# Order of transposes, scores and fillers in a stick-breaking attention loop, and of one projection's accumulators

## The chip, the cores and the metric

The kernel runs on one core of a Trainium2 chip. The core has a matrix engine (TensorE, PE in the profile, with PEld for its weight loads), a vector engine (VectorE, DVE), an activation engine (ScalarE, ACT), a general one (GpSimd, POOL), and a sync engine (SP) that issues most DMAs. The metric is the device time of one execution in microseconds (us); lower is better. The time before is the median of three runs.

## The reference

One layer of a model, in float32, with 1024 rows (positions) of width 1024. The input is normalised and modulated by a conditioning vector, then projected. Sixteen heads of 64 columns mix the positions: eight by forgetting attention (softmax with a decay) and eight by stick-breaking attention. Each is gated, and all go through one output projection, a gated residual and a last normalisation. The part that the change is about is the stick-breaking half:

```python
z = q @ k.T * scale                      # per head
strict = k_pos < q_pos
log_keep = where(strict, log_sigmoid(-z), 0.0)
later = cumsum(log_keep, reverse) - log_keep
w = where(strict, exp(log_sigmoid(z) + later), 0.0)
out = (w @ v) * silu(g)
```

Read as products, a weight is sigmoid(z) times the product of sigmoid(-z) over all later keys up to the query.

## The kernel before, in words

Heads are worked in eight pairs: 0 to 3 stick-breaking, 4 to 7 forgetting attention. A **unit** (p, h, i) is one head h of pair p and one block i of 128 queries, with its i+1 blocks of 128 keys. There are 16 units in a pair, 128 in all; `units` lists them and k counts them. Within pair 0 the order is blocks 0 to 3 of both heads and then 4 to 7 of both, so that units 8 to 15 are all wide. Float32 operands are split into a rounded high part and a low part, so that a product is two or three faster matrix products.

For a stick-breaking unit the steps are these.

- `att_scores` (L447): TensorE computes the scores into S, the only score buffer, in PSUM (L459, L460). ScalarE takes sigmoid(-z) as kp and sigmoid(z) as be (L481, L483), both reading S. VectorE scans kp from the end, in one or two pieces (L488, L492). GpSimd multiplies be by the shifted scan (L494) and clears the diagonal (L495). The function returns the last ScalarE and VectorE instructions of the unit.
- `att_query` (L428): a copy of the next unit's query block for the low-part product (L433).
- `att_transpose` (L499): TensorE transposes the weights by blocks of 128 into one or two groups of up to four, in buffers T (two of them, L511). ScalarE copies the high halves (L513), VectorE takes the low ones (L514); the last of these is kept in `lows`. Between the first and the second group, or behind the only one, it calls `att_pv` for pairs of units that are ready.
- `att_pv` (L521): the value products of two query blocks of a head into the one value buffer (L528), then the sums: a ScalarE copy (L535), two VectorE adds (L536, L537), GpSimd's product with the gate (L538) and a store.

The **fillers** are a chain of generators: the projections of later pairs (`gen_m`, `gen_v`), some small gate work, splitting the output weights, and the last gate projection (`gen_last_g`, L977). Each step of one issues some twelve wide-row value matmuls or six of 512 columns. `want` spreads the steps over the turns. Projections are accumulated in `acc` buffers, two of them in PSUM, which ScalarE and VectorE empty (`evac_m`). Weights come by DMA and are split on GpSimd (L126, L127).

The loop makes one **turn** per k. A turn issues scores of unit k, about half of its fillers, transposes of unit k-2 (LAG is 2) with value products, and the other fillers. Four turns also empty a part of the first projections that was held back in an SBUF tile (`HELD`: k = 4, 5, 6, 10; by `evac_q`, L265, or `evac_k`, L274, one head's half each). From turn 116 on the output projection is mixed in.

The order on TensorE is the program's. On ScalarE, VectorE and GpSimd a planner orders instructions by readiness and program order; `after(...)` (L83) makes a block's instructions stand behind the given ones on their engine.

Of the kernel before, what the change touches and what calls it, by code (L numbers as in the profile page):

```python
# [16 lines left out]
NB = 8  # L17
# [10 lines left out]
def tile_hybrid_layer(  # L28
# [33 lines left out]
    def acc_tile(name):  # L62
        return ps.tile([P, 512], F32, tag="acc", bufs=2, name=name)
# [19 lines left out]
    def after(*instructions):  # L83
        stack = ExitStack()
        for i in instructions:
            stack.enter_context(tc.issue_after(i.ins))
        return stack
# [177 lines left out]
    def evac_q(p, ch, acc, qst, heads):  # L265
        s = slice(ch * 512, ch * 512 + 512)
        for h in heads:
            r = slice(h * HD, h * HD + HD)
            o = slice((1 - h) * HD, (1 - h) * HD + HD)
            nc.scalar.activation(qst[h][r, s], acc[r, :], AF.Copy, scale=SCALE)  # L270
            nc.vector.scalar_tensor_tensor(qst[h][o, s], acc[r, :], SCALE, qst[h].bitcast(F32)[r, s],
                                           op0=ALU.mult, op1=ALU.subtract)

    def evac_k(p, ch, acc, kst, klo, heads):  # L274
        s = slice(ch * 512, ch * 512 + 512)
        for h in heads:
            r = slice(h * HD, h * HD + HD)
            o = slice((1 - h) * HD, (1 - h) * HD + HD)
            first = nc.scalar.copy(kst[h][r, s], acc[r, :])
            if ch == 1 and p in (2, 4, 6):  # L280
                key_casts[:] = [first]
            kf = kst[h].bitcast(F32)
            nc.sync.dma_start(kf[o, s], kf[r, s])
            last = nc.vector.tensor_tensor(klo[r, s], acc[r, :], kf[r, s], op=ALU.subtract)  # L284
        return first, last

    def evac_g(p, ch, acc, sg):
        s = slice(ch * 512, ch * 512 + 512)
        nc.scalar.activation(sg[:, s], acc, AF.Tanh, scale=0.5)
        nc.vector.scalar_tensor_tensor(sg[:, s], sg[:, s], 1.0, acc, op0=ALU.add, op1=ALU.mult)  # L290
# [22 lines left out]
    def evac_m(p, m, ch, acc, heads=(0, 1)):  # L313
        if m == 0:
            evac_q(p, ch, acc, qst[p], heads)
        elif m == 1:
            return evac_k(p, ch, acc, kst[p], klo[p], heads)
        else:
            evac_g(p, ch, acc, sgt[p])
# [115 lines left out]
    masks, scaled, lows = [], [], []  # L435

    def att_causal(u):
        p, h, i = u
        if p >= 4:
            if not masks:  # L440
                masks.append(pv_tile("causal_ps", 1)[:, :P])
                nc.vector.tensor_copy(masks[0], causal)
            f = fb[2 * (p - 4) + h]
            dg = slice(i * P, i * P + P)
            nc.vector.tensor_tensor(f[:, dg], f[:, dg], masks[0], op=ALU.add)
# [53 lines left out]
    def att_transpose(u, between=()):  # L499
        p, h, i = u  # L500
        a = st_w.pop(u)
        j, qo = i // 2, (i % 2) * P
        for g in range((i // 4) + 1):
            n = min(4, i + 1 - 4 * g)
            if (p, h, j, g) not in st_pt:
                st_pt[p, h, j, g] = pt_tile(f"pt_{p}_{h}_{j}_{g}", F32R, [P, 2, 4, 256])
            hi, lo = (st_pt[p, h, j, g][:, x] for x in range(2))
            tp = t_tile(f"T_{p}_{h}_{i}_{g}")
            for b in range(n):
                kb = 4 * g + b  # L510
                nc.tensor.transpose(tp[:, b * P:(b + 1) * P], a[:, kb * P:(kb + 1) * P], ident)  # L511
            t3 = tp[:, :n * P].rearrange("p (a b) -> p a b", a=n)
            nc.scalar.copy(hi[:, :n, qo:qo + P], t3)  # L513
            lows[:] = [nc.vector.tensor_tensor(lo[:, :n, qo:qo + P], t3, hi.bitcast(F32)[:, :n, qo:qo + P],  # L514
                                               op=ALU.subtract)]
            while between:
                att_pv(*between.pop(0))

    y_last = []

    def att_pv(p, h, j):  # L521
        acc = pv_tile(f"pv_{p}_{h}_{j}")
        last = 2 * j + 1
        acc2 = acc.rearrange("p (a b) -> p a b", a=2)
        for kb in range(last + 1):
            pt = st_pt[p, h, j, kb // 4][:, :, kb % 4]
            q0 = P if kb == last else 0
            nc.tensor.matmul(acc2[:, :, q0:], vt[p][:, kb, h * P:(h + 1) * P], pt[:, :, q0:],  # L528
                             start=(kb == 0), stop=(kb == last))
        r = slice(h * HD, h * HD + HD)  # L530
        o = slice((1 - h) * HD, (1 - h) * HD + HD)
        qs = slice(j * 256, j * 256 + 256)
        ty = sb.tile([P, 512], F32, tag="ty", bufs=2, name=f"ty_{p}_{h}_{j}")
        tm, yt = ty[:, :256], ty[:, 256:]
        nc.scalar.copy(tm[r, :], acc[o, :256])  # L535
        nc.vector.tensor_tensor(yt[r, :], acc[r, :256], tm[r, :], op=ALU.add)  # L536
        nc.vector.tensor_tensor(yt[r, :], acc[r, 256:], yt[r, :], op=ALU.add)  # L537
        nc.gpsimd.tensor_tensor(yt[r, :], yt[r, :], sgt[p][r, qs], op=ALU.mult)  # L538
        if p == NPAIR - 1:
            if not y_last:  # L540
                y_last.extend([big("sg", 2, "y7h", F32R), big("kl", 2, "y7l", F32R)])
            yh, yl = y_last
            nc.scalar.copy(yh[r, qs], yt[r, :])
            nc.gpsimd.tensor_tensor(yl[r, qs], yt[r, :], yh.bitcast(F32)[r, qs], op=ALU.subtract)
        else:
            nc.sync.dma_start(y_dr[p, r, qs], yt[r, :])
# [258 lines left out]
    for kb in range(NB):  # L805
# [9 lines left out]
        if kb < len(evacs):  # L815
            n, h = evacs[kb]
# [4 lines left out]
    held = att_tile("st_held")  # L821
# [31 lines left out]
    def load_wo(pr):  # L853
        hi = big(f"u{pr}", 1, f"woh_{pr}", F32R)
        lo = big(f"v{pr}", 1, f"wol_{pr}", F32R)
        nc.sync.dma_start(hi.bitcast(F32), wo_dr[0, pr])
        nc.sync.dma_start(lo.bitcast(F32), wo_dr[1, pr])
        wo[pr] = (hi, lo)
# [118 lines left out]
    def gen_last_g(p):  # L977
        tiles = fetch_m(p, 2)
        yield
        make_g(p)  # L980
        accs = [acc_tile(f"m_{p}_2_{ch}") for ch in range(2)]
        for kt in range(NB):
            for ch in (1, 0):
                m_step(accs[ch], tiles, kt, ch)
            if kt == NB - 1:
                for ch in (1, 0):
                    evac_m(p, 2, ch, accs[ch])
            load_wo(kt)
            yield

    fillers = chain([
# [10 lines left out]
    LEAD = 2  # L1002
    LAG = 2
# [4 lines left out]
    HELD = {4: (1, 1), 5: (0, 0), 6: (1, 0), 10: (0, 1)}  # L1008
# [4 lines left out]
    def fill(want):  # L1013
        while done[0] < want:
            done[0] += 1
            next(fillers, None)
# [10 lines left out]
    units = [u for p in range(NPAIR) for u in order(p)]  # L1027
    want = [0.0]
# [10 lines left out]
    seen = set()  # L1039
    ready = []  # L1040
    LAST = 16 * (NPAIR - 1)
    tail = chain([gen_out_first(6), gen_out_last(6)] + [gen_out(t) for t in OUT_ORDER[1:]])
    fill(2)
    for k in range(len(units) + LAG + 1):
        if k < len(units):
            if k == 16 * 4 - 1:
                load_fb(0)
                load_fb(1)
            if k == 0:
                att_query(units[0])  # L1050
            issued = att_scores(units[k], units[k + 1] if k + 1 < len(units) else None)
            if k == 16 * 4 - 1:
                att_causal(units[k + 1])
            if k + 1 < len(units):
                att_query(units[k + 1])
            p, h, i = units[k]
            if 4 <= p < NPAIR - 1 and i == 0:
                load_fb(2 * (p - 4) + h + 2)
        fill(want[2 * k + LEAD + 1])
        if LAG <= k < len(units) + LAG:  # L1060
            u = units[k - LAG]
            att_transpose(u, ready)
            if k in HELD:
                m, h = HELD[k]
                with after(*issued, *lows):
                    evac_m(0, m, 1, held[:, m * 512:(m + 1) * 512], (h,))
            seen.add(u)
            if (u[0], u[1], u[2] ^ 1) in seen:
                ready.append((u[0], u[1], u[2] // 2))
        while k >= len(units) + LAG and ready:  # L1070
            att_pv(*ready.pop(0))
        fill(want[2 * k + LEAD + 2])
        if k >= LAST + OUT0:
            for _ in range(TAIL[min(k - LAST - OUT0, len(TAIL) - 1)]):
                next(tail, None)
        if k == LAST:
            load_y(6)
            load_ln()
        for i, d in enumerate(YLOAD):
            if k == LAST + d:  # L1080
                load_y(OUT_ORDER[i + 1])
# [64 lines left out]
```

## Time and profile before

| | |
|---|---|
| median of three runs | 687.88 us (687.73 to 688.04) |
| the profiled execution | 687.36 us |
| its span, first to last instruction | 685.6 us |
| mean granted clock of TensorE | 0.997 |
| stick-breaking turns | from the first scores at 80.70 us to about 345 us |
| busy: DVE, ACT, POOL | 71%, 56%, 59% |

In the profile a row of a timeline gives the start in us, the length in us, the engine, the line of the kernel, the operation, what it writes and reads, the shapes and a count; a bracket at its end gives the time for which the engine stood idle ahead of it and what ended that. [...]

### The profile page before, as it was taken

How to read it: one execution, taken by the hardware profiler on the slowest of the kernel's cores; microseconds unless marked ns; L12 is line 12 of the kernel's file. 1: busy time of each engine (PE TensorE's matmuls, PEld its weight loads, DVE VectorE, ACT ScalarE, POOL GpSimd, SP SyncE). 2: the span in 40 equal slices, each digit the busy share in tenths (PEclk: the TensorE clock that was granted, in tenths of full speed). 3: DMA queues.
4: the chain of work that ended last, by engine and by line, in shares of the span. 5: the costliest groups of instructions: out<-in, count | busy, mean ns of one | idle time of the engine just before them, and what ended most of it. 6: DMA issues, size and time to landing. Idle time of an engine off the chain costs nothing.

```text
span 685.6 us, 11206 instructions
## 1 busy us (share of the span) xinstructions
PE 671.9 (98%) x3713; PEld 571.4 (83%) x3713; DVE 488.1 (71%) x996; ACT 381.5 (56%) x857; POOL 403.3 (59%) x529
## 2 busy tenths in 40 slices
PE   8999999999999999999999999999999999999995
PEld 5788888788998888889988888889988878888885
DVE  6697779867668777777776675766676777885645
ACT  6567378756568666566665564655565666521000
POOL 5560269756347565556368878777784365655411
PEclk9999999999999999999999999999999999999998
DMA  8973432112102122122123454254352297143301
GB/s 334 409 280 129 138 75 77 40 25 62 32 10 70 40 55 55 40 54 55 52 88 128 162 164 164 79 176 147 125 163 64 68 361 287 59 179 102 119 32 61
DMA packets 45272, 81.54 MB, mean 119 GB/s; under 512 B 5216, under 2 KB 19360, under 8 KB 44960
## 3 DMA queue, kind: packets, MB, share of 16 engines
q1 hardware_dynamic: 43632, 76.54, 33.7%
q10 hardware_dynamic: 1584, 4.31, 1.9%
q8 instruction: 29, 0.48, 0.3%
q14 instruction: 27, 0.22, 0.1%
HBM read 60.34 MB, written 16.29 MB: 112 GB/s over the span
## 4 chain that ended last, share of the span: by engine, by line
PE 85%; DVE 6%; ACT 3%; POOL 2%; issue 2%; DMA 1%; DVEq 0%; POOLq 0%; ACTq 0%
PE pv L528 9%; PE m L296 9%; PE m L298 9%; PE m L297 9%; PE T L511 8%; PE o L909 4%; PE o L908 4%; PE o L907 4%; PE S L460 4%; PE S L459 4%; PE v L356 4%; PE v L354 4%; PE v L355 3%; PE st_q L614 1%; PE st_late L614 1%
## 5 line engine op out<-in xcount | busy, mean ns | idle before, releaser
L296 PE MATMUL m<-uh,whi 128*128 128x512 f32 x304 | 125.0, 411 | 0.7 <-DVE kl L284 0.7
L514 DVE TENSOR_TENSOR pt<-T,pt 128x512 fp32r<-128x512 f32 (+2 forms) x192 | 103.2, 551 | 26.0 <-ACT pt L513 24.2
L298 PE MATMUL m<-uh,wlo 128*128 128x512 f32 x304 | 119.7, 394 | 0.0
L297 PE MATMUL m<-ul,whi 128*128 128x512 f32 x304 | 119.6, 394 | 0.0
L513 ACT CAST pt<-T 128x512 fp32r<-128x512 f32 (+2 forms) x192 | 88.7, 479 | 42.8 <-PE T L511 39.9
L494 POOL TENSOR_TENSOR be<-be,kp 128x127 f32<-128x127 f32 (+3 forms) x64 | 77.6, 1213 | 37.5 <-DVE kp L492 27.6
L488 DVE TENSOR_TENSOR_SCAN kp<-kp,floor 128x512 f32<-128x512 f32 (+2 forms) x64 | 65.1, 1018 | 28.5 <-ACT kp L481 25.4
L528 PE MATMUL pv<-pt,v 128*128 128x512 f32 x320 | 82.8, 388 | 0.3 <-DVE pt L514 0.3
L538 POOL TENSOR_TENSOR ty<-ty,sg 64x256 f32<-64x256 f32 x64 | 46.9, 733 | 42.7 <-DVE ty L537 18.3
L475 POOL TENSOR_SCALAR a<-a,l 128x1024 f32<-128x1024 f32 (+3 forms) x64 | 48.1, 752 | 39.6 <-DVE l L473 28.9
L298 PEld LDWEIGHTS m<-uh,wlo 128*128 128x128 f32 x304 | 57.1, 188 | 13.6
L459 PE MATMUL S<-k,q 128*128 128x512 f32 (+5 forms) x192 | 66.2, 346 | 0.3 <-DVE nm L467 0.2
L296 PEld LDWEIGHTS m<-uh,whi 128*128 128x128 f32 x304 | 57.2, 188 | 10.1 <-DVE kl L284 1.1
L460 PE MATMUL S<-kl,qz 128*128 128x512 f32 (+5 forms) x192 | 65.3, 341 | 0.0
L472 ACT ACTIVATE a<-a,nm 128x1024 f32<-128x1024 f32 (+3 forms) x64 | 49.8, 778 | 26.8 <-DVE nm L467 25.8
L297 PEld LDWEIGHTS m<-ul,whi 128*128 128x128 f32 x304 | 57.3, 189 | 7.9
L528 PEld LDWEIGHTS pv<-pt,v 128*128 128x128 f32 x320 | 55.4, 189 | 9.6 <-DVE pt L514 0.6
L481 ACT ACTIVATE kp<-S 128x128 f32<-128x128 f32 (+3 forms) x64 | 41.7, 652 | 33.6 <-PE S L460 31.2
L467 DVE CUSTOM_DVE_ANT_0 a<-S,fb 128x1024 f32<-128x1024 f32 (+3 forms) x64 | 48.3, 754 | 15.8 <-PE S L460 11.2
L433 ACT CAST qz<-q 64x128 fp32r<-64x128 f32 x128 | 37.2, 295 | 34.7 <-PE S L460 33.2
L354 PE MATMUL v<-whi_v,uh 128*128 128x256 f32 (+1 forms) x192 | 55.6, 289 | 0.0
L356 PE MATMUL v<-wlo_v,uh 128*128 128x256 f32 (+1 forms) x192 | 54.3, 283 | 0.0
(290 smaller groups left out, 1625.3 us busy)
## 6 DMA issues: line engine op xcount, KB each, us to landing
raw<-in_w_qkg_dram SPq DMA_DIRECT2D x38, 256.0 KB, 2.7
wss<-in_w_ss_dram SPq DMA_DIRECT2D x12, 512.0 KB, 8.4
x<-in_x_dram SPq DMA_DIRECT2D x8, 512.0 KB, 6.8
k<-k SPq DMA_DIRECT2D x32, 128.0 KB, 2.3
wg<-in_w_gate_dram SPq DMA_DIRECT2D x8, 512.0 KB, 4.6
raw_o<-in_w_out_dram SPq DMA_DIRECT2D x16, 256.0 KB, 3.0
fb<-f_dr ACTq DMA_DIRECT2D x8, 512.0 KB, 4.0
wo_dr<-whi_o SPq DMA_DIRECT2D x16, 256.0 KB, 2.2
```

Of the source, the lines that this page charges most:

```text
L296: nc.tensor.matmul(acc, hi[:, c], u_hi[kt][:, s], start=(kt == 0), stop=False)
L297: nc.tensor.matmul(acc, hi[:, c], u_lo[kt][:, s], start=False, stop=False)
L298: nc.tensor.matmul(acc, lo[:, c], u_hi[kt][:, s], start=False, stop=(kt == NB - 1))
L354: nc.tensor.matmul(acc[:, :n], u_hi[kt][:, ts_], hi[:, s], start=(kt == 0), stop=False)
L356: nc.tensor.matmul(acc[:, :n], u_hi[kt][:, ts_], lo[:, s], start=False, stop=(kt == NB - 1))
L459: nc.tensor.matmul(S[:, s, :w], qst[p][h][:, qs], kst[p][h][:, ks], start=True, stop=False)
L460: nc.tensor.matmul(S[:, s, :w], z, klo[p][:, ks], start=False, stop=True)
L488: last_dve = nc.vector.tensor_tensor_scan(rv, rv, floor[:, :ke - lo], initial=0.0, op0=ALU.mult, op1=ALU.max)
L494: nc.gpsimd.tensor_tensor(be[:, :ke - 1], be[:, :ke - 1], kp[:, 1:ke], op=ALU.mult)
L513: nc.scalar.copy(hi[:, :n, qo:qo + P], t3)
L514: lows[:] = [nc.vector.tensor_tensor(lo[:, :n, qo:qo + P], t3, hi.bitcast(F32)[:, :n, qo:qo + P], op=ALU.subtract)]
L528: nc.tensor.matmul(acc2[:, :, q0:], vt[p][:, kb, h * P:(h + 1) * P], pt[:, :, q0:], start=(kb == 0), stop=(kb == last))
```

## The change

Four things are altered. In turns below 64 (stick-breaking), the turn begins with the transposes of unit k-2 and the value products, then come the scores of unit k, then all fillers of the turn; from turn 64 on the order stays as it was. The output sums of a stick-breaking value product become a function of their own, `att_sum`; they are put on a list and issued after the next scores, behind that unit's last sigmoid and last scan. The held halves are emptied at the same place, ahead of these sums, behind the same instructions and no longer behind the last low half. In `gen_last_g` the accumulators are made in the order (1, 0), and the first two steps go to one accumulator each, two key blocks of it, in place of one key block of both; the loads of output weights keep their step.

```diff
+        if p < 4:
+            summed.append((acc, p, h, j))
+        else:
+            att_sum(acc, p, h, j)
+
+    def att_sum(acc, p, h, j):
         r = slice(h * HD, h * HD + HD)
...
-        accs = [acc_tile(f"m_{p}_2_{ch}") for ch in range(2)]
-        for kt in range(NB):
-            for ch in (1, 0):
+        accs = {ch: acc_tile(f"m_{p}_2_{ch}") for ch in (1, 0)}
+        for n in range(NB):
+            for kt, ch in ([(0, 1 - n), (1, 1 - n)] if n < 2 else [(n, 1), (n, 0)]):
                 m_step(accs[ch], tiles, kt, ch)
...
-            load_wo(kt)
+            load_wo(n)
             yield
...
+    def weights_turn(k):
+        if LAG <= k < len(units) + LAG:
+            u = units[k - LAG]
+            att_transpose(u, ready)
+            seen.add(u)
+            if (u[0], u[1], u[2] ^ 1) in seen:
+                ready.append((u[0], u[1], u[2] // 2))
+        while k >= len(units) + LAG and ready:
+            att_pv(*ready.pop(0))
+
+    def scores_turn(k):
         if k < len(units):
...
             issued = att_scores(units[k], units[k + 1] if k + 1 < len(units) else None)
...
+            if k in HELD:
+                m, h = HELD[k]
+                with after(*issued):
+                    evac_m(0, m, 1, held[:, m * 512:(m + 1) * 512], (h,))
+            with after(*(issued or ())):
+                while summed:
+                    att_sum(*summed.pop(0))
             if k + 1 < len(units):
                 att_query(units[k + 1])
...
-        fill(want[2 * k + LEAD + 1])
-        if LAG <= k < len(units) + LAG:
-            u = units[k - LAG]
-            att_transpose(u, ready)
-            if k in HELD:
-                m, h = HELD[k]
-                with after(*issued, *lows):
-                    evac_m(0, m, 1, held[:, m * 512:(m + 1) * 512], (h,))
...
+    for k in range(len(units) + LAG + 1):
+        if k < 16 * 4:
+            weights_turn(k)
+            scores_turn(k)
+        else:
+            scores_turn(k)
+            fill(want[2 * k + LEAD + 1])
+            weights_turn(k)
         fill(want[2 * k + LEAD + 2])
```

More of the change, by code (lines that the diff above doesn't have):

```diff
@@ L517, in att_transpose @@
                 att_pv(*between.pop(0))
-    y_last = []
+    y_last, summed = [], []
     def att_pv(p, h, j):
@@ L980, in gen_last_g @@
         make_g(p)
-        accs = [acc_tile(f"m_{p}_2_{ch}") for ch in range(2)]
-        for kt in range(NB):
-            for ch in (1, 0):
+        accs = {ch: acc_tile(f"m_{p}_2_{ch}") for ch in (1, 0)}
+        for n in range(NB):
+            for kt, ch in ([(0, 1 - n), (1, 1 - n)] if n < 2 else [(n, 1), (n, 0)]):
                 m_step(accs[ch], tiles, kt, ch)
-            if kt == NB - 1:
+            if n == NB - 1:
                 for ch in (1, 0):
                     evac_m(p, 2, ch, accs[ch])
-            load_wo(kt)
+            load_wo(n)
             yield
@@ L1043, in tile_hybrid_layer @@
     fill(2)
-    for k in range(len(units) + LAG + 1):
+    def weights_turn(k):
[8 more added lines that the diff above has]
+    def scores_turn(k):
         if k < len(units):
@@ L1058, in tile_hybrid_layer @@
                 load_fb(2 * (p - 4) + h + 2)
-        fill(want[2 * k + LEAD + 1])
-        if LAG <= k < len(units) + LAG:
-            u = units[k - LAG]
-            att_transpose(u, ready)
-            if k in HELD:
-                m, h = HELD[k]
-                with after(*issued, *lows):
-                    evac_m(0, m, 1, held[:, m * 512:(m + 1) * 512], (h,))
[L1067 to L1071, printed above, removed]
+    for k in range(len(units) + LAG + 1):
[6 more added lines that the diff above has]
+            weights_turn(k)
         fill(want[2 * k + LEAD + 2])
```

## The prediction

> **What bounds the kernel now.** I read the page first, then the chain of waits by engine, then stretches of the span, then the timeline at the places that these named. From the page:
>
> ```profile
> span 685.6 us, 11206 instructions
> PE 671.9 (98%) x3713; PEld 571.4 (83%) x3713; DVE 488.1 (71%) x996; ACT 381.5 (56%) x857; POOL 403.3 (59%) x529
> PE 85%; DVE 6%; ACT 3%; POOL 2%; issue 2%; DMA 1%; DVEq 0%; POOLq 0%; ACTq 0%
> ```
>
> TensorE is busy for 98% of the span and makes up 85% of the chain that ended last. The change adds and removes no matrix instruction, so it can only win time in which TensorE waits. What waits there are is in the view of waits, for PE alone:
>
> ```profile
> PE T L511 <- DVE pt L514: 1.8, 3, 1.4
> PE m L296 <- DVE kl L284: 0.7, 1, 0.7
> PE T L511 <- POOL be L494: 0.4, 1, 0.4
> PE pv L528 <- DVE pt L514: 0.3, 1, 0.3
> ```
>
> The columns are the total in us, the number of times, and the longest. The prize is small: 3.2 us of shown idle time. A matmul row lasts longer than its place in the queue, though, so part of each wait lies under the row before it. Start to start is the safer measure:
>
> ```profile
> 116.97 1.76 POOL L494 TENSOR_TENSOR be<-be,kp 128x895 f32<-128x895 f32 x1
> 117.08 0.81 PE L511 MATMUL T<-ident,be 128*128 128x128 f32 x6
> 117.22 2.06 DVE L271 SCALAR_TENSOR_TENSOR q<-st_held,q 64x512 fp32r<-64x512 f32 x1
> 118.21 1.02 ACT L483 ACTIVATE be<-S 128x1024 f32<-128x1024 f32 x1
> 118.67 0.40 PE L297 MATMUL m<-ul,whi 128*128 128x512 f32 x1
> 118.90 0.40 PE L298 MATMUL m<-uh,wlo 128*128 128x512 f32 x1
> 119.43 0.38 PE L459 MATMUL S<-k,q 128*128 128x320 f32 x1
> 121.03 1.28 DVE L492 TENSOR_TENSOR_SCAN kp<-kp,floor 128x512 f32<-128x512 f32 x1
> 121.24 0.39 PE L298 MATMUL m<-uh,wlo 128*128 128x512 f32 x1
> 122.22 1.00 DVE L514 TENSOR_TENSOR pt<-T,pt 128x512 fp32r<-128x512 f32 x2
> 123.04 0.63 PE L511 MATMUL T<-ident,be 128*128 128x128 f32 x4 [1.41 <-DVE pt L514]
> ```
>
> Two matmuls of 512 columns start 0.23 us apart (118.67 and 118.90). After the one at 121.24 the transposes should start at 121.47; they start at 123.04, so 1.57 us are lost where the bracket shows 1.41: a wait costs its bracket and 0.16 more. The rows tell why. The six transposes at 117.08 fill both T buffers. Their low halves (L514) are taken by VectorE only at 122.22, because the held query half (L271) and then two scans are ahead of them in its queue; the next transposes need a T buffer back. A second loss stands at 118.90: the scores at 119.43 start 0.30 us late, since the sigmoid L483 still reads the one S buffer until 119.23.
>
> **What the change wins.** In the first four pairs the transposes of unit k-2 and any finished value product now come ahead of the scores of unit k, so T is copied and its low half taken before that unit's sigmoids and scans queue up. The output sums go behind the scan, and the held halves too, both after the scores. By these rows the three T waits go: 1.8 + 3 x 0.16 = 2.3 us. The value product that waited for the low half of the unit before it has a whole turn now instead of a part: 0.3 + 0.16 = 0.5. The S wait goes, because scores now have the whole filler and the transposes behind them before the next scores: 0.3. I leave the wait on the product L494 (0.4) as it is: it comes of no order that is changed. Sum 3.1.
>
> The gate projection, from the timeline:
>
> ```profile
> 549.55 0.39 PE L298 MATMUL m<-uh,wlo 128*128 128x512 f32 x1
> 549.87 0.69 DVE L284 TENSOR_TENSOR kl<-m,k 64x512 fp32r<-64x512 f32 x1 [0.15 <-ACT k L279]
> 550.62 0.50 PE L296 MATMUL m<-uh,whi 128*128 128x512 f32 x1 [0.68 <-DVE kl L284]
> 551.67 0.48 PE L296 MATMUL m<-uh,whi 128*128 128x512 f32 x1
> ```
>
> Three matmuls go into the first accumulator, and the fourth wants the second, which the key evacuation holds until 550.56 (549.87 + 0.69). It starts at 550.62 instead of 549.78: 0.84 lost. With six into the first accumulator the second is wanted about 0.7 us later and behind three transposes, by when it is free: 0.8 won. The load of the first output weights now waits one step longer for its buffer on SP's queue, about 2 us, and the load of the second stands with it; nothing needs them before the output projection, which no wait in the PE list names, so this costs nothing. If that cover were gone, it would cost those 2 us.
>
> Transposes cost the instruction behind them a little: the projection matmul at 551.67 lasts 0.48 where the one at 549.55 lasts 0.39, and a wide score product in the same place lasts 0.48 too (the row at 204.78 below). Scores now stand behind them and projections no longer do; one price takes the place of the other, so the sum is nil. Gains: 3.1 + 0.8 = 3.9 us.
>
> **What it costs.** From the scores of unit k to its transposes, sigmoid, scan and GpSimd's product must fit. That cover was two turns and the first half of a third; now it is two turns less the transposes of turn k. If nothing waits, T(k) starts where S(k+2) started before, since the same instructions stand ahead of it, and S(k) starts later by the T and value products of its own turn. First the narrowest place, unit 8 (pair 0, five key blocks):
>
> ```profile
> 107.82 0.49 PE L511 MATMUL T<-ident,be 128*128 128x128 f32 x3
> 108.50 0.33 PE L459 MATMUL S<-k,q 128*128 128x384 f32 x1
> 108.67 0.48 DVE L492 TENSOR_TENSOR_SCAN kp<-kp,floor 128x128 f32<-128x128 f32 x1
> 109.34 0.61 POOL L126 TENSOR_SCALAR whi<-raw 128x512 fp32r<-128x512 f32 x1
> 109.95 1.31 POOL L494 TENSOR_TENSOR be<-be,kp 128x639 f32<-128x639 f32 x1
> 111.10 0.47 PE L459 MATMUL S<-k,q 128*128 128x448 f32 x1
> ```
>
> The transposes and values of turn 8 take 108.50 - 107.82 = 0.7 us. The weights' product ended at 109.95 + 1.31 = 111.26; put 0.7 later it ends at 111.9, and T(8) wants it at 111.10. So 0.8 is short. But the scan had ended at 109.15 and the product stood behind a weight split on GpSimd until 109.95, so up to 0.8 can come back. Between 0 and 0.8 I take 0.5. Unit 10, two turns later:
>
> ```profile
> 113.41 0.60 PE L511 MATMUL T<-ident,be 128*128 128x128 f32 x4
> 114.66 0.27 PE L511 MATMUL T<-ident,be 128*128 128x128 f32 x1
> 114.81 1.01 DVE L492 TENSOR_TENSOR_SCAN kp<-kp,floor 128x384 f32<-128x384 f32 x1
> 115.70 1.30 POOL L127 TENSOR_TENSOR wlo<-raw,whi 128x512 fp32r<-128x512 f32 x1
> ```
>
> The work put ahead of its scores takes about 1.3 us (113.41 to 114.66, and the last transpose). The product ended at 116.97 + 1.76 = 118.73, so 120.0 with the shift, against 119.43: 0.6 short, of which the split at 115.70 (the scan ended at 115.82, the product began at 116.97) could give back 1.1. I take 0.3. Behind it VectorE is full, as the stretches show (busy us of PE, PEld, DVE, ACT, POOL):
>
> ```profile
> 105.00:115.00 10.00, 10.00 (x62) 8.82 (x61) 9.20 (x15) 8.00 (x17) 9.78 (x14) 1.00 0.34 93
> 115.00:125.00 10.00, 8.46 (x44) 6.63 (x43) 9.77 (x13) 7.04 (x16) 6.60 (x8) 1.00 0.13 36
> 210.00:280.00 70.00, 69.41 (x356) 57.76 (x355) 52.64 (x80) 47.70 (x102) 45.04 (x62) 1.00 0.19 51
> ```
>
> VectorE works 9.2 and 9.8 of 10 us there and GpSimd 9.8 in the first; turn 12 has to take its values' accumulator back from the sums that now stand behind scan and held half. Between nothing and the 1.57 lost at this place before, I take 0.4. In all 1.2 us of new waits in pair 0. In pairs 1 to 3 VectorE has a quarter of its time free (52.6 of 70), and the cover is wide. The narrowest that I found among them:
>
> ```profile
> 203.49 0.60 PE L511 MATMUL T<-ident,be 128*128 128x128 f32 x4
> 204.78 0.48 PE L459 MATMUL S<-k,q 128*128 128x512 f32 x1
> 206.21 1.77 POOL L494 TENSOR_TENSOR be<-be,kp 128x895 f32<-128x895 f32 x1
> 210.62 0.22 PE L459 MATMUL S<-k,q 128*128 128x128 f32 x1
> ```
>
> The product ends at 207.98; the transposes put ahead take 204.78 - 203.49 = 1.3, and T may start at 210.62: 1.3 us are left. I cost these pairs at nothing; that is lost if their chains grow by more than 1.3 us.
>
> The held query half of turn 10 bears on this. By line 271 the two held query halves are one form:
>
> ```profile
> L271 DVE SCALAR_TENSOR_TENSOR q<-st_held,q x2: 687/1372/2057, 100.4 to 117.2; 64x512 fp32r<-64x512 f32 x2
> ```
>
> One took 0.69 us (shortest, mean of the two and longest stand in ns), the one at 117.22 took 2.06. Both its reads are in SBUF, and it ended at 119.28, 0.55 after GpSimd's product, begun just before it, ended at 118.73. So it lost 1.4 to that product. [...]
>
> **Sum.** 3.9 won, 1.2 lost: 2.7 us less. The profiled execution took 687.36 us, its span of 685.6 and 1.8 around it, so 684.7; the median of the three runs is 687.88, 0.5 above it, so 685.2 there, and I say 685.1. A measurement of this kernel can hardly tell less than 0.2% (1.4 us) from no change: faster begins below 686.5, slower above 689.3.
>
> **Rivals.** *All waits go* (0.13): the split on GpSimd falls elsewhere, and the new waits come to nothing. 687.9 - 3.9 = 684.0, and 683.4 if the wait on L494 (0.4 + 0.16) goes as well. For it: the earlier low halves relieve VectorE's queue. Against: GpSimd at 9.78 of 10.
>
> *Pair 0 is bound by VectorE and GpSimd, not by order* (0.20): the 1.57 + 0.5 + 0.3 won there come back as waits of T for the product, and of the 3.9 only 1.5 remain, of which the 0.5 at T(8) is still paid: 1.0 won, 686.9. For it: 9.77 of 10 at the loss. Against: 2.06 of that was one instruction that waited.
>
> [...]
>
> *It does not do what it says* (0.07): the planner orders VectorE's queue itself; if it keeps scans ahead of low halves, the T waits stay, and the gate alone gives 687.1.
>
> *Slower* (0.10): the low halves and copies now run just when sigmoid and scan want to. If the two copies and two low halves of a wide unit (the low halves 1.00 at 122.22; the copies, by estimate from that row of as many elements, 0.9) all go ahead of its chain, that chain grows by 1.9 us. It decides from the 1.3 us of cover above. In pair 0 the shortage would be 1.9 at every second wide unit (two are in flight, and a stall for one covers the other), four times: 7.6, less the 3.9 won: 3.7, about 691.5. Against it: the transposes end before the scores begin, and 0.9 us of score matmuls (four, 0.23 apart) and a sigmoid of 1.0 (as at 118.21) run before the first scan can start.
>
> **The numbers.** My forecast has 0.42. Range: 683.0 (all waits go, and 0.4 for what the list of waits may not show) to 689.0, which takes in both rivals near no change and the mild half of the slower one; the forecast's own is 684.2 to 686.3. Faster: 0.42 + 0.13 + half of the port and a little of the VectorE rival, 0.62. Slower: 0.11. The same: 0.27.
>
> **What would show it.** Right: no T wait for L514 in the first four pairs; no wait of m for L284 near 550; L514 ahead of L488 in each turn; a wait of T for L494 near 111 and 119, of about half a microsecond. Wrong: T waits for L494 in pairs 1 to 3, or waits of over 2 us in pair 0, or of pv for the sums L537.

## The result, and the profile after

The changed kernel takes 685.2 us (median of six runs, 684.96 to 685.56) beside 687.92 (six runs) for the kernel before. The ratio is 0.9958, with a 95% interval of 0.9948 to 0.9969: 2.7 us won. The profiled execution took 685.27 us, its span 683.2.

From the page of the changed kernel, the busy times and the engines of its chain:

```profile
PE 670.8 (98%) x3713; PEld 571.9 (84%) x3713; DVE 485.1 (71%) x996; ACT 379.1 (55%) x857; POOL 404.6 (59%) x529
PE 91%; DVE 2%; POOL 2%; ACT 2%; issue 1%; DMA 1%; SPq 0%; DVEq 0%; POOLq 0%; ACTq 0%
```

TensorE does the same 3713 products, and its part of the chain that ended last went from 85% to 91%, while VectorE's fell from 6% to 2%: a matrix instruction now seldom stands behind VectorE. The waits of TensorE that the change made, moved or left, in the changed kernel:

```profile
PE v L356 <- POOL wlo_v L127: 0.8, 1, 0.8
PE T L511 <- POOL be L494: 0.4, 1, 0.4
```

No wait for a low half (L514) is left, and none of m for the key evacuation (L284). One wait of T for the weights' product (L494) stands there as before, though in another place. New is the first line, a value projection that waits for its split weights. The list has one more wait that the list before has not, 0.8 at 12 us (xT_early, L242, for ScalarE); the kernels are alike up to there, and in the traces of all runs it lies between nothing and 1.0, so it is taken as chance.

Comparing the start of each turn's first matmul between the two traces gives the sum by place. The two start 0.4 apart, for the chance wait at 12 us. Then, in us (a minus sign is time won): turns 6 to 7 -0.56, T(7) +0.17, T(8) +0.54, to turn 13 -1.64, around 175 -0.42, around 212 -0.63, at the forget-gate work behind it +0.31 and +0.14, around 246 -0.35; the rest are steps of less than 0.2. At turn 64 the changed kernel is 2.2 ahead, so the loop won 2.6. The gate projection won another 0.80, and 0.7 to 0.8 were lost at 457 us.

The timeline of the changed kernel where the kernel before lost most:

```profile
109.04 0.48 DVE L492 TENSOR_TENSOR_SCAN kp<-kp,floor 128x128 f32<-128x128 f32 x1
109.58 0.61 POOL L126 TENSOR_SCALAR whi<-raw 128x512 fp32r<-128x512 f32 x1
110.19 1.31 POOL L494 TENSOR_TENSOR be<-be,kp 128x639 f32<-128x639 f32 x1
110.79 0.39 PE L298 MATMUL m<-uh,wlo 128*128 128x512 f32 x1
111.56 0.66 PE L511 MATMUL T<-ident,be 128*128 128x128 f32 x4 [0.38 <-POOL be L494]
117.37 0.69 DVE L271 SCALAR_TENSOR_TENSOR q<-st_held,q 64x512 fp32r<-64x512 f32 x1
117.42 2.28 POOL L494 TENSOR_TENSOR be<-be,kp 128x895 f32<-128x895 f32 x1 [0.31 <-DVE kp L492]
119.01 1.02 DVE L514 TENSOR_TENSOR pt<-T,pt 128x512 fp32r<-128x512 f32 x2
119.32 0.40 PE L298 MATMUL m<-uh,wlo 128*128 128x512 f32 x1
119.85 0.63 PE L511 MATMUL T<-ident,be 128*128 128x128 f32 x4
119.95 1.21 DVE L488 TENSOR_TENSOR_SCAN kp<-kp,floor 128x512 f32<-128x512 f32 x1
```

The low halves at 119.01 now stand ahead of the scan L488 at 119.95; before, they came behind both scans at 122.22. Two small waits were paid for it. T(8) should start at 110.79 + 0.23 = 111.02 and starts at 111.56: 0.54. T(10) should start at 119.55 and starts at 119.85: 0.30. Both wait for GpSimd's product, but for different reasons. At T(8) a weight split (L126) lies between the scan, which ended at 109.52, and the product at 110.19. At T(10) the product itself lasted 2.28 where 1.76 were shown before: it began 0.05 behind the held half L271.

The gate projection in the changed kernel: the sixth product into the first accumulator, the transposes, the second accumulator.

```profile
548.65 0.39 PE L298 MATMUL m<-uh,wlo 128*128 128x512 f32 x1
548.88 0.49 PE L511 MATMUL T<-ident,a 128*128 128x128 f32 x3
549.26 0.51 PE L296 MATMUL m<-uh,whi 128*128 128x512 f32 x1
```

Nothing stands idle between them. The place that got worse, first in the changed kernel, then in the one before:

```profile
456.95 0.28 PE L355 MATMUL v<-whi_v,ul 128*128 128x256 f32 x1
458.05 0.39 PE L356 MATMUL v<-wlo_v,uh 128*128 128x256 f32 x1 [0.82 <-POOL wlo_v L127]
```

```profile
459.29 0.28 PE L355 MATMUL v<-whi_v,ul 128*128 128x256 f32 x1
459.62 0.38 PE L356 MATMUL v<-wlo_v,uh 128*128 128x256 f32 x1
```

Two such products follow each other 0.12 apart when nothing waits. They are 1.10 apart after and 0.33 before, so about 0.8 of the win is given back here: TensorE comes 2.3 us earlier to the first of them, and the split of the value weights only 1.6. Its high part starts at 456.02, after GpSimd has waited 0.57 for the DMA to land; before, it started at 457.57, right behind GpSimd's split ahead of it.

The stretch of the changed kernel that answers to the fullest one shown before:

```profile
115.00:125.00 10.00, 9.87 (x52) 8.07 (x51) 9.73 (x13) 8.92 (x18) 7.26 (x8) 1.00 0.21 60
```

VectorE is as full in it as before (9.73 of 10, and 9.77), and TensorE now works 9.87 of it where it worked 8.46. VectorE's load was not what held it.

### The profile page after: what moved, and what is told of

Read it like the earlier page. It is cut to its first block, busy times and chain, and to the rows that moved or that the text cites. A ratio compares the mean times of both kernels' runs of the same rounds, so it can differ in the third digit from the quotient of the medians.

```text
span 683.2 us, 11185 instructions
## 1 busy us (share of the span) xinstructions
PE 670.8 (98%) x3713; PEld 571.9 (84%) x3713; DVE 485.1 (71%) x996; ACT 379.1 (55%) x857; POOL 404.6 (59%) x529
## 4 chain that ended last, share of the span: by engine, by line
PE 91%; DVE 2%; POOL 2%; ACT 2%; issue 1%; DMA 1%; SPq 0%; DVEq 0%; POOLq 0%; ACTq 0%
PE m L296 10%; PE m L298 10%; PE m L297 9%; PE pv L528 9%; PE T L511 9%; PE S L459 5%; PE S L460 5%; PE o L915 4%; PE o L913 4%; PE o L914 4%; PE v L356 4%; PE v L354 4%; PE v L355 4%; PE st_q L620 1%; PE st_late L620 1%
## 5 line engine op out<-in xcount | busy, mean ns | idle before, releaser
L514 DVE TENSOR_TENSOR pt<-T,pt 128x512 fp32r<-128x512 f32 (+2 forms) x192 | 102.8, 552 | 31.6 <-ACT pt L513 30.0
L296 PE MATMUL m<-uh,whi 128*128 128x512 f32 x304 | 122.8, 404 | 0.0
L494 POOL TENSOR_TENSOR be<-be,kp 128x127 f32<-128x127 f32 (+3 forms) x64 | 78.4, 1226 | 37.0 <-DVE kp L492 23.9
L488 DVE TENSOR_TENSOR_SCAN kp<-kp,floor 128x512 f32<-128x512 f32 (+2 forms) x64 | 65.0, 1015 | 26.3 <-ACT kp L481 25.1
L459 PE MATMUL S<-k,q 128*128 128x512 f32 (+5 forms) x192 | 69.4, 363 | 0.3 <-DVE nm L467 0.2
L467 DVE CUSTOM_DVE_ANT_0 a<-S,fb 128x1024 f32<-128x1024 f32 (+3 forms) x64 | 48.2, 753 | 16.2 <-PE S L460 12.0
L355 PE MATMUL v<-whi_v,ul 128*128 128x256 f32 (+1 forms) x192 | 54.1, 282 | 0.0
```

The costliest lines, as they stand in the source:

```text
L296: nc.tensor.matmul(acc, hi[:, c], u_hi[kt][:, s], start=(kt == 0), stop=False)
L355: nc.tensor.matmul(acc[:, :n], u_lo[kt][:, ts_], hi[:, s], start=False, stop=False)
L459: nc.tensor.matmul(S[:, s, :w], qst[p][h][:, qs], kst[p][h][:, ks], start=True, stop=False)
L494: nc.gpsimd.tensor_tensor(be[:, :ke - 1], be[:, :ke - 1], kp[:, 1:ke], op=ALU.mult)
```

## The experiments

Theory: the order of the instructions makes the gain, because low halves taken ahead of the scans give T back in time; putting off the sums and held halves only shortens the chain to the product. Rival: the relief of VectorE's queue by putting them off makes it, wherever the transposes stand. Behind that stand the questions what the small waits left in pair 0 are, and how near the slower rival is.

**The gate projection alone** (the kernel before, with the new `gen_last_g`):

```diff
-        accs = [acc_tile(f"m_{p}_2_{ch}") for ch in range(2)]
+        accs = {ch: acc_tile(f"m_{p}_2_{ch}") for ch in (1, 0)}
...
-            for ch in (1, 0):
+            for kt, ch in ([(0, 1 - n), (1, 1 - n)] if n < 2 else [(n, 1), (n, 0)]):
```

> The kernel before with the new order of the last gate projection's accumulators alone. My theory: the one wait for the key evacuation near 550 us (0.84 us from start to start) goes and nothing else moves: 0.8 us less than before, about 687.1. Rival (what is won there is given back, since the loads of the output weights wait a step longer): no change, 687.9.

Measured: 687.1 (686.62 to 688.08) beside 688.01; ratio 0.9989 [0.998, 0.9998]: 0.9 won. The wait of m for L284 is gone.

**The loop alone** (the changed kernel with the old `gen_last_g`; the diff above reversed):

> The change without the new accumulator order. My theory: the waits of transposes for VectorE's low halves go, about half a microsecond each comes back at units 8 and 10; from the trace of after the turns of the first four pairs should end 2.6 us earlier against their own start: 685.4 to 686.0, with the 0.8 us wait near 550 us back. If the wait for the split value weights near 457 us (0.8 us in after) is part of the new pace it is there again; if it is chance it is not. Rival (the gate makes most of the gain): 687.1.

Measured: 686.14 (685.53 to 686.4); ratio 0.9971 [0.9959, 0.9982]: 1.9 won. 1.9 + 0.9 = 2.8 beside the 2.7 of both: the two parts add up.

**The order alone** (the loop alone, with sums at once and held halves behind the last low half issued):

```diff
-        if p < 4:
-            summed.append((acc, p, h, j))
-        else:
-            att_sum(acc, p, h, j)
+        att_sum(acc, p, h, j)
...
-                with after(*issued):
+                with after(*issued, *lows):
```

> Transposes and values first, then scores, then fillers; but the output sums are issued at once with their value products, and the held halves stand behind the last low half again. Old gate order. Theory A (the order does it, the sums' place is a detail): 685.4 to 686.2. Theory B (the sums and held halves ahead of the scan lengthen the chain, whose cover is now short): the waits of transposes for the product at units 8, 10 and 12 grow by the two sums (0.8 us) each, 1.5 to 2.5 us in all, and the time is 687 to 688.

Measured: 686.5 (686.19 to 686.99); ratio 0.9977 [0.9968, 0.9986]: 1.5 of the loop's 1.9. Its timeline ahead of T(8):

```profile
108.41 0.43 DVE L540 TENSOR_TENSOR ty<-pv,ty 64x256 f32<-64x256 f32 x1
111.06 0.39 PE L298 MATMUL m<-uh,wlo 128*128 128x512 f32 x1
111.52 1.31 POOL L494 TENSOR_TENSOR be<-be,kp 128x639 f32<-128x639 f32 x1
112.89 0.66 PE L511 MATMUL T<-ident,be 128*128 128x128 f32 x4 [1.44 <-POOL be L494]
```

The two sums, of which this is the second, stand ahead of unit 8's scan, which starts at 108.87; the product follows late (111.52, and 110.19 in the change), and T(8) loses 112.89 - 111.29 = 1.60 in place of 0.54. The held half is not moved by its condition: the last low half that is issued by then belongs to T(8) and is long done, so L271 starts at 118.70, right behind the scan as in the change, the product beside it lasts 2.27, and T(10) loses 0.20. This run thus prices the putting off of the sums alone. It is worth 1.07 at T(8), but between the traces of the two runs as much goes again further on (0.10 at T(10), 0.31 at the forget gate, 0.56 at 457 us, 0.23 at the gate projection). In the medians it is 0.4, and the runs overlap a little.

**The putting off alone** (the loop alone, with the old order in every turn):

```diff
-        if k < 16 * 4:
-            weights_turn(k)
-            scores_turn(k)
-        else:
-            scores_turn(k)
-            fill(want[2 * k + LEAD + 1])
-            weights_turn(k)
+        scores_turn(k)
+        fill(want[2 * k + LEAD + 1])
+        weights_turn(k)
```

> The old order of scores, fillers, transposes, fillers; but sums and held halves go behind the next unit's scan. Old gate order. Theory A (the order does it): the waits of transposes for low halves stay, since the scans still stand ahead of the low halves: 687.5 to 688.3. Theory B (the wait of 1.57 us came of the held half of turn 10 alone): that one goes, 686.3.

Measured: 692.87 (691.95 to 693.27); ratio 1.0068 [1.0054, 1.0081]: 4.9 slower than before. No theory had this. In its timeline, in pair 3:

```profile
279.82 1.28 DVE L492 TENSOR_TENSOR_SCAN kp<-kp,floor 128x512 f32<-128x512 f32 x1
282.31 0.43 DVE L543 TENSOR_TENSOR ty<-pv,ty 64x256 f32<-64x256 f32 x1
282.77 1.02 DVE L514 TENSOR_TENSOR pt<-T,pt 128x512 fp32r<-128x512 f32 x2
283.61 0.63 PE L511 MATMUL T<-ident,be 128*128 128x128 f32 x4 [1.15 <-DVE pt L514]
```

In the old order the low halves come behind the scan, which ends at 281.10, and now two sums of 0.43 stand between as well (the second is shown), beside an evacuation of 0.69: the low halves start at 282.77, some 0.9 later than without the sums. T waits for low halves six times, for 3.7 in all, where before it was three times and 1.8, and for GpSimd's product 1.5, where before it was 0.4. By place, pair 0 comes out about even: the 1.57 falls by 0.86, with the held half now 0.69 long in place of 2.06, but 0.8 is lost just ahead of it. Pairs 1 to 3 lose 4.6. So putting off alone wins nothing; it lengthens just the queue that T waits for. The rival falls.

**Scores first** (the changed kernel with scores, then transposes and values, then all fillers):

```diff
-            weights_turn(k)
             scores_turn(k)
+            weights_turn(k)
```

> The change, but each of the first 64 turns issues the scores first, the transposes and values right behind them, then all fillers. Theory A (the transposes must come ahead of the scores, so that their low halves are ahead of the scans): the copies now compete with the sigmoids and the low halves with the scans of the same turn, and the next transposes, a turn later, find T buffers late as in the kernel before: waits for low halves, 688 to 691. Theory B (what counts is only that all fillers lie between): 685.2 to 685.8.

Measured: 706.94 (704.53 to 707.54); ratio 1.0268 [1.0252, 1.0285]: 19 slower, several times the size that was expected of the order. Its longest waits:

```profile
PE T L511 <- DVE pt L514: 8.6, 7, 2.1
PE pv L528 <- DVE ty L543: 4.4, 5, 2.4
PE pv L528 <- DVE pt L514: 2.0, 2, 1.8
```

These are 15.0, and 14 times 0.16 beside the brackets 2.2. The rest is in the granted clock, in the column behind the five busy times:

```profile
112.54:115.95 3.41, 1.57 (x10) 1.13 (x9) 3.29 (x6) 3.36 (x6) 3.33 (x5) 1.00 0.29 84
115.95:119.36 3.41, 3.41 (x11) 2.73 (x10) 2.84 (x5) 0.88 (x4) 3.33 (x4) 0.50 0.32 75
122.78:126.19 3.41, 1.64 (x8) 0.92 (x6) 3.31 (x4) 3.36 (x8) 0.97 (x2) 1.00 0.01 2
126.19:129.60 3.41, 3.03 (x10) 2.58 (x11) 3.35 (x7) 1.34 (x3) 1.96 (x3) 0.50 0.08 18
```

Twice, behind 3.41 us of which TensorE has worked only about half (1.57 and 1.64), the clock stands at half for 3.41 us. In the first of these places the 512-column matmuls start 0.43 apart in place of 0.23. TensorE works 3.41 and 3.03 us in the two; an estimate from these rows, with half of that work as lost, is 3.2. 15.0 + 2.2 + 3.2 = 20.4, beside 21.9 between the spans; the other 1.5 is not followed up.

**The held half one turn earlier** (`HELD` with `9: (0, 1)` in place of `10: (0, 1)`):

> The change, with the last held half (second head's queries) taken at turn 9 in place of 10. In after, VectorE's instruction on it takes 0.69 us right behind the scan of unit 10, GpSimd's product of that unit takes 2.28 in place of 1.76, and its transposes wait 0.3 and their value product 0.2. [...] Theory B (VectorE is simply full there): the waits stay or move to unit 9's transposes: 685.2.

Measured: 685.73 (684.82 to 686.28); ratio 0.9966 [0.9954, 0.9978]. That is between the 685.2 of the change and the 685.97 of its repeat below. The product of unit 10 and, earlier, the held half in its timeline:

```profile
113.51 0.69 DVE L271 SCALAR_TENSOR_TENSOR q<-st_held,q 64x512 fp32r<-64x512 f32 x1
113.57 1.11 POOL L126 TENSOR_SCALAR whi<-raw 128x512 fp32r<-128x512 f32 x1
117.46 1.77 POOL L494 TENSOR_TENSOR be<-be,kp 128x895 f32<-128x895 f32 x1
```

The product of unit 10 lasts 1.77 again and T(10) has no wait, so the held half was what lengthened it. But the half now lengthens the weight split beside it, 1.11 in place of 0.61. The 0.3 is too small to be seen in these medians.

**The split behind the product** (the changed kernel, with two high splits ordered behind the products of units 8 and 10):

```diff
+            product = nc.gpsimd.tensor_tensor(be[:, :ke - 1], be[:, :ke - 1], kp[:, 1:ke], op=ALU.mult)
+            products[:] = [product] if u in BEHIND_PRODUCT else []
...
+        with after(*products):
+            nc.gpsimd.tensor_scalar(hi[:, :n], raw, 1.0, 1.0, op0=ALU.mult, op1=ALU.mult)
```

> The change, with the weight splits that are fetched in the fillers of turns 8 and 10 ordered behind GpSimd's product of that turn's unit. In after the product of unit 8 starts 0.67 us behind its scan, with a split in between, and the transposes wait 0.54. Theory A (GpSimd's order costs that wait): it goes, 0.5 less than the change, about 684.7. Theory B (the chain itself is too long): product 8 starts earlier and the wait shrinks by no more than 0.2, or the later splits make projections wait for weights: 685.2 to 686.

Measured: 690.92 (690.31 to 691.51); ratio 1.0042 [1.003, 1.0055]: 5.7 slower than the change. T(8) no longer waits for the product, but the projections ahead of it wait for the weights; the waits and two stretches:

```profile
PE m L301 <- POOL wlo L130: 2.1, 1, 2.1
PE m L299 <- POOL whi L129: 2.1, 1, 2.1
```

```profile
110.71:114.12 3.41, 0.73 (x2) 0.30 (x2) 2.70 (x4) 0.60 (x3) 3.21 (x6) 1.00 0.06 13
114.12:117.53 3.41, 3.24 (x10) 2.65 (x11) 0.00 (x0) 0.27 (x1) 3.21 (x4) 0.50 0.28 88
```

4.2 + 2 x 0.16 of waits and, by the same estimate, 3.24 / 2 = 1.6 of clock, less the 0.54: 5.6, beside 5.4 between the traces. Split and product are both due at that moment, and GpSimd can't do both in time.

**A longer chain in pairs 1 to 3** (one GpSimd operation more behind each product there, times one in place):

```diff
+            for _ in range(1 if 0 < p < 4 else 0):
+                nc.gpsimd.tensor_scalar(be[:, :ke - 1], be[:, :ke - 1], 1.0, 1.0, op0=ALU.mult, op1=ALU.mult)
```

> The change, with one more GpSimd instruction behind the weights' product of each unit of pairs 1 to 3 (a multiplication of the weights by one in place, 0.3 to 0.8 us by width), so that each chain from scores to transposes is longer by it. Theory A (the cover there is at least 1.3 us): no transposes wait for it, 685.2 to 685.5. Theory B (the shortened cover is already near its end, the slower rival): waits of transposes for the product at the wide units, 0.3 to 0.6 us each at a dozen of them: 688 to 691.

Measured: 692.11 (691.85 to 692.3); ratio 1.0059 [1.0045, 1.0073]: 6.9 slower than the change, with new waits of T for GpSimd. Unit 38 in it, and in the changed kernel:

```profile
243.07 1.77 POOL L494 TENSOR_TENSOR be<-be,kp 128x895 f32<-128x895 f32 x1 [0.17 <-DVE kp L492]
244.80 1.30 POOL L127 TENSOR_TENSOR wlo<-raw,whi 128x512 fp32r<-128x512 f32 x1
246.77 0.94 POOL L496 TENSOR_SCALAR be<-be 128x895 f32<-128x895 f32 x1
247.77 0.65 PE L513 MATMUL T<-ident,be 128*128 128x128 f32 x4 [0.95 <-POOL be L497]
```

```profile
239.63 1.77 POOL L494 TENSOR_TENSOR be<-be,kp 128x895 f32<-128x895 f32 x1 [0.16 <-DVE kp L492]
243.22 0.60 PE L511 MATMUL T<-ident,be 128*128 128x128 f32 x4
```

The planner put a split (at 244.80) and the gate product of an output sum (0.73) ahead of the added operation, so the chain grew by 247.71 - 244.84 = 2.9 and not by 0.94; the run doesn't price one operation. What it does give is a cover: the changed kernel's product ends at 241.40 and T starts at 243.22, 1.8 later. 2.9 - 1.8 = 1.1, and the wait is 0.95 + 0.16 = 1.11. The slower rival's mechanism is real, and begins at 1.8 us in this place.

The last three were measured side by side. **The change again**:

> The change itself, beside the next two on the same chip. Both theories: 685.2, a ratio of about 0.996 to the kernel before. Its profile shows whether the wait of 0.8 us for the split value weights near 457 us belongs to the change's pace (then it is there again) or to chance.

Measured: 685.97 (684.7 to 686.29); ratio 0.9965 [0.9951, 0.9978]. Here the change wins 1.8, not 2.7: two of the five runs took 684.7 and 684.9, three 686.0 to 686.3. The wait at 457 us came again, with 0.6. The trace, of the slowest of these runs, has one more:

```profile
557.46 0.50 PE L459 MATMUL S<-k,q 128*128 128x512 f32 x1 [0.90 <-DVE nm L467]
```

VectorE had waited 1.25 us until 554.87 for a DMA (of fb, for L445), so its work on the score buffer, L467, ended late, and 1.10 are lost against the first trace of the change. The same DMA is late by less, and 0.4 and 0.3 are lost at this product, in the traces of the gate alone and of the held half at turn 9.

**Four splits on ScalarE** (the changed kernel; high parts only):

```diff
+        if key in ('1_2_0', '1_2_1', '2_0_0', '2_0_1'):
+            nc.scalar.copy(hi[:, :n], raw)
+        else:
+            nc.gpsimd.tensor_scalar(hi[:, :n], raw, 1.0, 1.0, op0=ALU.mult, op1=ALU.mult)
```

> The change, with the rounding of four weight pieces that are used around turns 7 to 11 (their high parts, 0.62 us each) moved from GpSimd to ScalarE; their low parts stay on GpSimd. Theory A (the transposes of unit 8 wait because GpSimd is full at 9.8 of 10 us there): its product starts right behind the scan and the wait of 0.54 goes, about 0.5 less than the change: 684.7. Theory B (the chain of scores, sigmoid, scan and product is itself too long for the cover): the wait stays at 0.3 or more, and ScalarE's added work delays the sigmoids: 685.2 to 685.6.

Measured: 684.34 (684.01 to 684.51); ratio 0.9949 [0.9936, 0.9961]. The interval overlaps that of the change, but each of its runs lies below each of the repeat's: 1.6 between the medians. Unit 8 in it:

```profile
109.76 1.32 POOL L497 TENSOR_TENSOR be<-be,kp 128x639 f32<-128x639 f32 x1 [1.05 <-DVE kp L495]
111.30 0.60 PE L514 MATMUL T<-ident,be 128*128 128x128 f32 x4
```

GpSimd stands idle when the scan ends and the product starts with it, at 109.76 where the change has 110.19; T(8) has no bracket, and starts right in its place behind the projections. Against the repeat's trace T(8) wins 0.54, of which 0.24 is given back around it (T(7) and the scores behind T(8), 0.12 each), 0.2 is won at 457 us, and 1.1 is the wait at 557 us, which this trace has not and which the moved splits are not shown to remove. Against the first trace of the change, which has no wait at 557 either, the span is 0.6 shorter. It has the lowest median here.

**Both together** (splits on ScalarE and the held half at turn 9):

> Both: the four high parts on ScalarE, and the last held half at turn 9. Theory A: no wait of over 0.2 us is left between 80 and 345 us but the one at the forget gate; 0.8 less than the change by the trace, about 684.4, the fastest so far. Theory B: VectorE is at 9.7 of 10 us there and takes the time back: 685.2.

Measured: 684.7 (684.45 to 685.2); ratio 0.9955 [0.9942, 0.9967]. It isn't the fastest, and its waits aren't gone:

```profile
114.31 0.69 DVE L274 SCALAR_TENSOR_TENSOR q<-st_held,q 64x512 fp32r<-64x512 f32 x1
114.36 2.05 POOL L497 TENSOR_TENSOR be<-be,kp 128x767 f32<-128x767 f32 x1 [0.16 <-DVE kp L495]
120.32 0.66 PE L514 MATMUL T<-ident,be 128*128 128x128 f32 x4 [0.47 <-POOL be L497]
```

With the split gone from GpSimd, the held half meets the product of unit 9, and T(10), one product later, loses 0.47 + 0.16 = 0.63.

## Why the prediction was right, point by point

The forecast was 2.7 us less, and 2.7 came, with 685.2 beside the 685.1 that was said (1.8 in the repeat). By its steps:

- **The waits in the loop.** Put at 3.1; 1.57 + 0.30 at turns 10 to 12, 0.56 at turn 7, 0.42 and 0.35 in later pairs make 3.2. Shown by cause as well: the order with the sums at once gives most of it, the putting off alone none. The sign that was named for it came too: L514 stands ahead of L488 in each turn of the first four pairs.
- **The wait for the product, left standing.** Wrong, in the safe direction. It stood at 212.83 in the kernel before:

```profile
210.73 2.00 POOL L494 TENSOR_TENSOR be<-be,kp 128x1023 f32<-128x1023 f32 x1 [0.50 <-DVE kp L492]
212.83 0.63 PE L511 MATMUL T<-ident,be 128*128 128x128 f32 x4 [0.43 <-POOL be L494]
```

  The step said that this wait comes of no order that is changed. But its transposes now stand at the head of the turn after, and 0.63 went. The wait of 0.4 in the list after is another, T(8)'s.
- **T(8), 0.5.** Right in size (0.54) and in cause: the split between scan and product, as the experiment with the splits on ScalarE shows.
- **T(10), 0.3.** Right in size (0.30) by luck, for the step's reason was another. The step let the product end late by the shift alone, at 120.0. It began at 117.42, 0.45 later than before, and lasted 0.52 longer beside the held half. The step had not asked what the product takes beside the held half: the held half took 0.69 and not 2.06, and it was GpSimd's product that took longer. The sum of the chances counts half of a port; no run shows a port, and what the traces show there is these two side by side, with 1.4 more on the held half in the kernel before and 0.52 more on the product after.
- **Turn 12, 0.4.** Not seen. The step feared that VectorE at 9.8 of 10 us would hand back the value accumulator late; it is as full as that after, and nothing waits. T(7) lost 0.17 instead.
- **Pairs 1 to 3 at nothing.** Nearly: the covers held, but +0.31 and +0.14 were lost at the forget-gate work. In the trace the first of them is a wait for the score buffer, of the kind that the step on gains had called gone: scores due at about 214.9 start at 215.18, behind the sigmoid L483, which ended at 215.14, with two table loads of 1.28 around the forget gate's work ahead of it on ScalarE. In the order before, these scores came 5.7 us behind those of the unit before them, and found the sigmoid done; now they are due 3.9 us behind. The cause of the second was not followed up.
- **The gate.** 0.8 forecast, 0.80 in the trace, 0.9 by its own run. The load behind it cost nothing.
- **The step that is missing.** Nothing in the prediction asked what the new order would run into further on. At 457 us it ran into weights that a DMA and a split bring at their own time, and lost 0.7 to 0.8. The size changes from run to run: 0.8 in three experiments' traces, 0.6 in the repeat, 0.3 to 0.5 in the other runs of the new order but the one with scores first, and 0.4 too in the run of the gate alone, which keeps the old pace up to there. The run with the split behind the product reaches this place 2.9 us later than the kernel before (462.18 and 459.29) and yet waits 0.8. So being early is not what makes the wait; its cause stays open, for no run moved the DMA alone. The wait at 557 us in the repeat is a second one for a DMA, and the gate alone, with the old loop, has a part of it too.

The loop's sum, 1.9 forecast and 1.9 measured, is thus 2.6 in the loop less the loss at 457: two terms missed upward (0.63 and 0.4) stand against two missed downward (0.45 at the forget gate, 0.7 at 457). The mechanism was right; that the total came out so close is in part luck. The rivals: pair 0 was bound by order and not by load, as the window from 115 to 125 shows; the slower one needs a chain that is longer by 1.8 us at unit 38, where the prediction had found 1.3 at its narrowest place.

## What to carry to other kernels

When one engine is 98% busy, read from its start-to-start times what each wait costs, and from the queue of the engine that it waits for what stands ahead of the release: here moving that release ahead of long instructions in the queue won 1.5 us by itself, and putting other work off in front of the release lost 4.9. Then ask what the engine meets further on, where weights come at their own time. And work out beside which instructions of the other engines a moved one will run, and where it stands in its queue: three of these experiments cured one wait and made another.

## What was unexpected of the hardware

**Who pays when the held half meets GpSimd's work.** Before, the held half took 2.06 in place of 0.69, so it lost 1.4 us, beside a GpSimd product that had begun 0.25 ahead of it (116.97 and 117.22). After, the held half begins first, takes its 0.69, and the product beside it, 0.05 later, lasts 2.28 in place of 1.77 for 895 columns. With the half at turn 9 it is the split, begun 0.06 later, that lasts 1.11 in place of 0.61; with the splits on ScalarE as well it is the product of 767 columns, begun 0.05 later, with 2.05 in place of 1.55. In these three the later one takes 0.50 to 0.51 more, and before it was the later one too. What lets one hold up the other, no run shows.

**Waits that cost twice.** In the run with the split behind the product the granted clock stood at half for 3.41 us once, and in the one with scores first twice, by the rows shown there; by the estimates there this added 1.6 and 3.2 us. The length of a wait does not decide it: the falls came beside waits of 1.84 to 2.15, and a wait of 2.39 with scores first left the clock at 1.00, in this stretch:

```profile
184.22:187.63 3.41, 2.06 (x13) 1.88 (x14) 2.07 (x8) 0.64 (x3) 2.88 (x4) 1.00 0.00 0
```

The two falls with scores first, at 115.95 and 126.19, lie 10.24 apart, three times 3.413, and the row above ends 21 times 3.413 behind the first. Counted in such stretches, TensorE had worked 1.57, 1.64 and 0.73 of the 3.41 us ahead of the falls, and 2.06 in the row above. The kernel before has a fall at 681.26, where its matrix work has ended. Counted back from there, TensorE had worked 0.63 in the stretch ahead of the fall (677.85 to 681.26); of all the others at full clock the one with the wait of 1.41 has the least work, 2.00 (121.48 to 124.89), and the clock stays at 1.00 in it and behind it. So of the stretches named here those with 0.63 to 1.64 us of TensorE's work were followed by half clock, and those with 2.00 and 2.06 were not; what decides between them, no run shows.
